# Decoder layer with a large expert table: PSUM banks, a DMA queue, buffers and the pace of the gate changed in the expert stage

## The chip, the cores and the metric

The kernel runs on one core of a Trainium2 chip, in one launch. The metric is the time of an execution on the device in microseconds (us), as the median of several executions. A profile of one execution shows what each engine did: TensorE (PE; PEld is its weight load), VectorE (DVE), ScalarE (ACT), GpSimd (POOL), SyncE (SP), and the 16 DMA engines.

## The reference: what is computed

One decoder layer on 512 tokens of width 1024: an attention part with two kinds of heads, a LayerNorm, and an expert part ("PEER") with a second LayerNorm. The change is in the expert part alone. There each token has 8 heads; each head picks 16 of 16384 experts, whose up and down vectors are rows of two tables:

```python
def peer(h, w_pq, sub_keys, u_tab, v_tab):
    def chunk(hx):                                       # 128 tokens
        q = (hx @ w_pq).reshape(PEER_CHUNK, PEER_HEADS, 2, PEER_HALF)
        sc = jnp.einsum('thpd,hpnd->thpn', q, sub_keys)
        v_half, i_half = lax.top_k(sc, PEER_TOPK)        # 16 of 128, twice
        ...                                              # 256 sums of pairs
        top_s, top_pos = lax.top_k(cand, PEER_TOPK)
        idx = jnp.take_along_axis(cand_idx, top_pos, axis=-1)
        g = jax.nn.softmax(top_s, axis=-1)
        a = jax.nn.gelu(jnp.einsum('thkd,td->thk', u_tab[idx], hx), approximate=False)
        return jnp.einsum('thk,thkd->td', (g * a).astype(hx.dtype), v_tab[idx])
```

## The kernel before, in words

Tokens are in four tiles of 128. The attention part, the first LayerNorm and the scores for the selection fill the first 374 us or so; the change touches them only through the number of raw buffers.

The expert part mixes two ways of computing. **Gathered:** for tile 0 wholly, and for the up part of tile 1, GpSimd fetches the chosen rows with indirect DMAs (`fetch`, 512 KB each, 384 in all, six buffers `gb`), and VectorE multiplies and adds them (L748, L764). **Dense:** for the other tiles all 16384 experts are computed, in 128 blocks of 128 experts. `u_block(e)` makes the up activations of one block for 256 tokens: 512 KB of `u_T` into a raw buffer (`load_raw`, 3 buffers, SP's queue); for even e a split into two parts, `hi` on ScalarE (L82) and `lo` on VectorE (L83), and 24 matmuls; for odd e 8 matmuls from `raw` (L783); all into a PSUM bank `st`, of which there are two (L779). ScalarE then writes GELU(`st`) to a slot `a_r` of a ring (L790). The ring has NB + 1 = 33 slots.

Three stages follow each other:

- **Up stage.** `u_block(e)` for e = 0 to NB + NS - 1 = 103. The first NB = 32 activations stay in the ring. The next NS = 72 are stored to HBM by `keep` (a DMA `a_d<-a_r`, 128 KB, SP's queue), which frees their slot. Between the blocks stand the selection (`all_topk`, VectorE), gathers, and the gate (`all_g`, `make_g`): a weight for each token and expert, made from one-hot rows. One gate step is 16 one-hot products: 8 scalings on ScalarE (`go`, L683), 8 matmuls into two banks `acc` (L687), 2 copies to `stage` (L690); after two steps 1 MB goes to HBM (`g_d<-stage`). There are 48 steps; for each block GRATE = 0.62 of them are placed, the last 16 only when the gathers of tile 1 are done.
- **Up and down stage.** `v_block(n)` with `v_mm` is the down part: 512 KB of `v_blk`, split into `hi` and `lo`, times the activation weighted by the gate (`w`, `wh`, `wl`), 18 matmuls into six banks `acc`. Down blocks 0 to 23 alternate with the up blocks 104 to 127. Every eighth block `g_load` fetches 1.5 MB of gate for eight blocks (`gl`, two buffers, runs of 512 bytes), on SP's queue (L829).
- **Down stage.** Down blocks 24 to 127. The stored activations come last; each is read back (`a_b<-a_d`, two buffers, SP's queue).

Six PSUM banks `acc` and two `st` come from one pool from the up stage to the end. Instructions are placed in the engines' queues by a scheduler that goes by the order in the code, by the buffers that are free and by its own costs. Each queue is worked off in its order: an instruction that waits holds up all behind it, and SP's queue is the one that issues nearly all plain DMAs.

## Time and profile before

| | us |
|---|---|
| median of 3 executions (1716.8 to 1725.07) | 1720.55 |
| the profiled execution | 1716.91 |
| its span, first to last instruction | 1715.1 |
| TensorE busy (mean granted clock 0.935) | 1462.7 |
| VectorE busy | 1257.6 |
| ScalarE busy | 737.5 |
| GpSimd busy | 553.6 |

Busy times are unions over the span and overlap each other. The profile's transfers are 472.56 MB, 276 GB/s over the span: 269.82 MB on the one hardware queue (all issued by SP), 201.35 MB on the software queue (GpSimd's gathers). A share of DMA is the mean over the 16 engines.

### The profile page before, as it was taken

The numbers are of one execution on the slowest core, as the hardware profiler recorded it, in microseconds if no ns is written. First come the engines' busy times: TensorE is split into PE (matmuls) and PEld (weight loads), VectorE is DVE, ScalarE is ACT, GpSimd is POOL, SyncE is SP. The second block draws the span as 40 slices with busy tenths as digits, with TensorE's granted clock in tenths as the row PEclk, the third lists the DMA queues.
The fourth block names the chain that finished last, engine by engine and source line by source line (L and its number), as shares of the span: only waits on it lengthen the run. The fifth ranks groups of instructions, "written<-read, shape, count | busy, mean of one in ns | idle before, by whom it ended". The sixth has DMA issues, their size and how long they took to land.

```text
span 1715.1 us, 21754 instructions
## 1 busy us (share of the span) xinstructions
PE 1462.7 (85%) x7269; PEld 1226.5 (72%) x7269; DVE 1257.6 (73%) x2787; ACT 737.5 (43%) x1452; POOL 553.6 (32%) x402
## 2 busy tenths in 40 slices
PE   6999898997788789787878798799898778887997
PEld 5777687886677678676767686688676666665885
DVE  7787567999999777745666277567787677787867
ACT  2555534332377767662676421223333222332441
POOL 0000000005544343534344145343455345565000
PEclk9999899998899989998999999899899888998999
DMA  8765433227898899989898899898898999999852
GB/s 300 271 209 169 163 123 101 84 87 272 311 318 312 279 341 338 349 333 324 283 336 299 322 348 375 283 333 307 306 324 315 357 318 328 338 338 314 257 178 77
DMA packets 187042, 472.56 MB, mean 276 GB/s; under 512 B 15921, under 2 KB 84913, under 8 KB 183730
## 3 DMA queue, kind: packets, MB, share of 16 engines
q1 hardware_dynamic: 131634, 269.82, 46.2%
q0 software_dynamic: 55296, 201.35, 32.2%
q8 instruction: 57, 0.93, 0.2%
q14 instruction: 55, 0.45, 0.1%
HBM read 431.26 MB, written 39.85 MB: 275 GB/s over the span
## 4 chain that ended last, share of the span: by engine, by line
DMA 32%; PE 30%; DVE 17%; ACT 12%; issue 7%; SPq 1%; POOL 0%; DVEq 0%; ACTq 0%; POOLq 0%
DMA a_d<-a_r 11%; DMA raw<-v_blk 9%; DMA a_b<-a_d 6%; ACT go L683 4%; DVE acc L764 4%; PE bank L92 4%; PE bank L93 4%; PE bank L94 4%; PE st L783 4%; DMA raw<-u_T 3%; DVE lo L83 3%; PE acc L93 3%; PE acc L94 3%; PE acc L92 3%; ACT stage L690 2%
## 5 line engine op out<-in xcount | busy, mean ns | idle before, releaser
L734 POOL DMA_INDIRECT gb<-u_tab,ei x256 | 338.7, 1323 | 589.2 <-DVE gb L748 354.4
L83 DVE TENSOR_TENSOR lo<-raw,hi 128x1024 fp32r<-128x1024 f32 x211 | 257.5, 1221 | 216.8 <-ACT hi L82 213.1
L82 ACT CAST hi<-raw 128x1024 fp32r<-128x1024 f32 x211 | 220.8, 1048 | 379.1 <-DMA raw<-v_blk 217.5
L783 PE MATMUL st<-h2f,raw 128*128 128x256 f32 x1200 | 302.2, 405 | 79.0 <-ACT a_r L790 60.3
L92 PE MATMUL acc<-hi,wh 128*128 128x512 f32 x768 | 313.8, 409 | 39.3 <-ACT hi L82 35.1
L93 PE MATMUL acc<-lo,wh 128*128 128x512 f32 x768 | 311.6, 406 | 32.6 <-DVE lo L83 32.4
L783 PEld LDWEIGHTS st<-h2f,raw 128*128 128x128 f32 x1200 | 237.8, 204 | 120.9 <-ACT a_r L790 67.1
L748 DVE SCALAR_TENSOR_TENSOR gb<-gb,h2n 128x1024 f32<-128x1024 f32 x256 | 305.4, 1220 | 5.5 <-DMA gb<-u_tab,ei 3.6
L94 PE MATMUL acc<-hi,wl 128*128 128x512 f32 x768 | 308.3, 401 | 0.0
L734 POOL DMA_INDIRECT gb<-v_tab,ei x128 | 204.9, 1601 | 191.6 <-DVE acc L764 139.0
L92 PEld LDWEIGHTS acc<-hi,wh 128*128 128x128 f32 x768 | 150.2, 196 | 75.8 <-ACT hi L82 38.9
L93 PEld LDWEIGHTS acc<-lo,wh 128*128 128x128 f32 x768 | 150.1, 195 | 73.2 <-DVE lo L83 40.4
L94 PEld LDWEIGHTS acc<-hi,wl 128*128 128x128 f32 x768 | 150.0, 195 | 31.4
L683 ACT ACTIVATE go<-oh,iT 128x128 f32<-128x128 bf16 x384 | 167.6, 526 | 2.7 <-DVE oh L677 2.0
L92 PE MATMUL st<-h2h,hi 128*128 128x256 f32 x424 | 133.3, 314 | 35.1 <-ACT a_r L790 34.2
L764 DVE SCALAR_TENSOR_TENSOR acc<-gb,w,acc 128x1024 f32<-128x1024 f32 x127 | 162.5, 1279 | 0.0
L94 PE MATMUL st<-h2h,lo 128*128 128x256 f32 x424 | 130.3, 307 | 12.2 <-DVE lo L83 12.2
L100 POOL TENSOR_TENSOR rs_r<-rs_v,mhalf 128x1 f32<-128x1 f32 (+1 forms) x12 | 9.3, 775 | 373.5 <-DVE rs_v L98 319.2
L93 PE MATMUL st<-h2l,hi 128*128 128x256 f32 x424 | 126.8, 299 | 0.0
L92 PEld LDWEIGHTS st<-h2h,hi 128*128 128x128 f32 x424 | 88.3, 208 | 43.3 <-ACT a_r L790 41.1
L687 PE MATMUL acc<-go,oh 128*128 128x128 f32 x768 | 107.7, 287 | 7.0 <-ACT go L683 7.0
L687 PEld LDWEIGHTS acc<-go,oh 128*128 128x128 f32 x768 | 98.8, 195 | 16.1 <-ACT go L683 8.7
(212 smaller groups left out, 2090.6 us busy)
## 6 DMA issues: line engine op xcount, KB each, us to landing
raw<-u_T SPq DMA_DIRECT2D x128, 512.0 KB, 6.3
raw<-v_blk SPq DMA_DIRECT2D x128, 512.0 KB, 6.3
wada<-w_adaT SPq DMA_DIRECT2D x48, 512.0 KB, 4.5
g_d<-stage SPq DMA_DIRECT2D x24, 1024.0 KB, 7.1
gl<-g_d SPq DMA_DIRECT2D x16, 1536.0 KB, 15.2
a_d<-a_r SPq DMA_DIRECT2D x72, 128.0 KB, 4.9
a_b<-a_d SPq DMA_DIRECT2D x72, 128.0 KB, 5.1
raw<-w_pqT SPq DMA_DIRECT2D x16, 512.0 KB, 3.6
```

Of the source, the lines that this page charges most:

```text
L82: nc.scalar.copy(hi, src)
L83: split.last = nc.vector.tensor_sub(lo, src, hi.bitcast(F32))
L92: nc.tensor.matmul(ps, lh, rh, start=first, stop=False)
L93: nc.tensor.matmul(ps, lh, rl, start=False, stop=False)
L94: nc.tensor.matmul(ps, ll, rh, start=False, stop=last)
L683: nc.scalar.activation(go[:, i, :], oh0[:, :, i], AF.Copy, scale=iT[:, 2, t0 + i:t0 + i + 1])
L687: nc.tensor.matmul(ps[:, i * P:(i + 1) * P], oh1[:, 4 * u + i, :], go[:, 4 * u + i, :], start=True, stop=True)
L690: nc.scalar.copy(stage[:, :, w:w + 4].rearrange("p i t -> p t i"), ps.rearrange("p (t i) -> p t i", t=4))
L734: nc.gpsimd.indirect_dma_start(out=b, out_offset=None, in_=A[tab], in_offset=bass.IndirectOffsetOnAxis(ap=ei[:, j:j + 1], axis=0))
L748: paced(nc.vector.scalar_tensor_tensor(b, b, 1.0, h2n, op0=OP.mult, op1=OP.mult, accum_out=dots[:, j:j + 1]))
L764: paced(nc.vector.scalar_tensor_tensor(acc0, b, w[:, j:j + 1], acc0, op0=OP.mult, op1=OP.add))
L783: nc.tensor.matmul(ps, raw[:, k, :], h2f[:, k, :], start=k == 0, stop=k == KB - 1)
```

## The change

Five edits in one. While the up stage runs, the PSUM pool has four banks `st` and four `acc`; after it that pool is closed, and a new one has two and six, as before. The gate load is issued on ScalarE's queue. Raw buffers are four instead of three, buffers for activations that are read back three instead of two. The ring keeps 24 activations instead of 32, so 80 are stored instead of 72 (the up stage still has 104 blocks). GRATE is 0.75.

```diff
-NB = 32
+NB = 24
 GB = 8
-NS = 72
-GRATE = 0.62
+NS = 80
+GRATE = 0.75
...
-        raw = stream.tile(shape, F32, name="raw", tag="raw", bufs=3)
+        raw = stream.tile(shape, F32, name="raw", tag="raw", bufs=4)
...
-    psB = ctx.enter_context(tc.tile_pool(name="psB", bufs=1, space=bass.MemoryType.PSUM, reuse_waits="tile"))
+    psB_stack = ExitStack()
+    psq = [psB_stack.enter_context(tc.tile_pool(name="psB", bufs=1, space=bass.MemoryType.PSUM, reuse_waits="tile")), 4, 4]
...
-        return psB.tile([P, 512], F32, name="acc", tag="acc", bufs=6)
+        return psq[0].tile([P, 512], F32, name="acc", tag="acc", bufs=psq[2])
...
-        ps = psB.tile([P, TU], F32, name="st", tag="st", bufs=2)
+        ps = psq[0].tile([P, TU], F32, name="st", tag="st", bufs=psq[1])
...
     sel_stack.close()
+    psB_stack.close()
+    psq[:] = ctx.enter_context(tc.tile_pool(name="psC", bufs=1, space=bass.MemoryType.PSUM, reuse_waits="tile")), 2, 6
...
-        dma(gl, g_d.rearrange("g p i t -> p g (i t)")[:, :, e * TG:(e + GB) * TG])
+        nc.scalar.dma_start(gl, g_d.rearrange("g p i t -> p g (i t)")[:, :, e * TG:(e + GB) * TG])
...
-            a = vp.tile([P, TU], F32, name="a_b", tag="a_b", bufs=2)
+            a = vp.tile([P, TU], F32, name="a_b", tag="a_b", bufs=3)
```

Where instructions move, at three places. The number behind a tile's name only tells tiles of one kind apart.

SP's queue around the store of block 60, which is `a_d28` before and `a_d36` now (the number counts the stores). Before, with `raw_6526` the weights of block 65:

```order
L88 DMA raw_6460<-u_T 128x1024
L694 DMA g_d_155<-stage_6215 128x2048
L795 DMA a_d28_111<-a_r_6321 128x256
L88 DMA raw_6526<-u_T 128x1024
L795 DMA a_d29_112<-a_r_6341 128x256
L88 DMA raw_6546<-u_T 128x1024
L795 DMA a_d30_113<-a_r_6407 128x256
```

Now, with `raw_6640` the weights of block 66 and `raw_6680` those of block 67:

```order
L88 DMA raw_6640<-u_T 128x1024
L796 DMA a_d36_119<-a_r_6467 128x256
L695 DMA g_d_163<-stage_6407 128x2048
L88 DMA raw_6680<-u_T 128x1024
L796 DMA a_d37_120<-a_r_6513 128x256
L88 DMA raw_6697<-u_T 128x1024
L796 DMA a_d38_121<-a_r_6553 128x256
```

Loads and stores alternate as before; the load ahead of a store is that of the sixth block after it instead of the fourth.

ScalarE's queue at the turn from the up stage to the down blocks. Before, with `a_r_8001` and `a_r_8130` the GELUs of blocks 100 and 103, `stage_8047` the last piece of the gate:

```order
L790 ACTIVATE a_r_8001<-st_7970 128x256
...
L790 ACTIVATE a_r_8110<-st_8079 128x256
L790 ACTIVATE a_r_8130<-st_8119 128x256
L690 COPY stage_8047<-acc_8146 128x4x128
L690 COPY stage_8047<-acc_8152 128x4x128
L82 CAST hi_8256<-raw_8254 128x1024
```

Now, with `a_r_8029`, `a_r_8095` and `a_r_8172` the GELUs of blocks 99, 100 and 103, `stage_7946` the last piece of the gate, `gl_8196` the first gate load:

```order
L791 ACTIVATE a_r_8029<-st_8018 128x256
L691 COPY stage_7946<-acc_8045 128x4x128
L691 COPY stage_7946<-acc_8051 128x4x128
L82 CAST hi_8222<-raw_8220 128x1024
L791 ACTIVATE a_r_8095<-st_8064 128x256
L832 DMA gl_8196<-g_d_163 128x24x128
L791 ACTIVATE a_r_8112<-st_8101 128x256
L82 CAST hi_8276<-raw_8274 128x1024
L832 DMA gl_8624<-g_d_163 128x24x128
L791 ACTIVATE a_r_8152<-st_8121 128x256
L791 ACTIVATE a_r_8172<-st_8161 128x256
```

The last copies of the gate have moved ahead by four GELUs, and the first two gate loads stand between the GELUs.

The sixth gate load (for down blocks 40 to 47). Before, in SP's queue, between weights of down blocks; `raw_9805` is that of down block 33:

```order
L88 DMA raw_9728<-v_blk 128x1024
L88 DMA raw_9770<-v_blk 128x1024
L829 DMA gl_10062<-g_d_155 128x24x128
L88 DMA raw_9805<-v_blk 128x1024
L88 DMA raw_9843<-v_blk 128x1024
```

Now, in ScalarE's queue, with `gl_9480` and `gl_9780` the gates of the blocks before:

```order
L855 CAST wh_9756<-gl_9480 128x128
L856 CAST wh_9756<-w_9754 128x256
L82 CAST hi_9712<-raw_9710 128x1024
L832 DMA gl_10082<-g_d_163 128x24x128
L82 CAST hi_9750<-raw_9748 128x1024
L855 CAST wh_9798<-gl_9780 128x128
```

It stands behind the last cast that reads the gate in its own buffer, `gl_9480`, and ahead of the cast of the next block's weights; SP's queue holds only weights there.

## Rows read from the trace of the kernel before

**Rows 1.** Stages: busy us (instructions) of PE, PEld, DVE, ACT, POOL; clock, DMA share, GB/s.

```profile
374.00:541.00 167.00, 136.78 (x769) 120.77 (x769) 154.19 (x485) 89.31 (x148) 74.63 (x55) 0.91 0.79 286
541.00:976.00 435.00, 344.18 (x2082) 309.94 (x2081) 277.63 (x434) 271.62 (x515) 180.26 (x133) 0.93 0.89 321
976.00:1182.00 206.00, 184.21 (x793) 153.79 (x792) 129.93 (x241) 46.80 (x102) 80.39 (x67) 0.94 0.95 330
1182.00:1592.00 410.00, 343.29 (x1385) 273.58 (x1384) 316.14 (x450) 123.99 (x232) 208.31 (x130) 0.90 0.93 324
```

**Rows 2.** The page's chain that ended last, by line, share of the span.

```profile
DMA a_d<-a_r 11%; DMA raw<-v_blk 9%; DMA a_b<-a_d 6%; ACT go L683 4%; DVE acc L764 4%; PE bank L92 4%; PE bank L93 4%; PE bank L94 4%; PE st L783 4%; DMA raw<-u_T 3%; DVE lo L83 3%; PE acc L93 3%; PE acc L94 3%; PE acc L92 3%; ACT stage L690 2%
```

**Rows 3.** Stores `a_d`, 541 to 976 us: issues, who waited, issue to landing.

```profile
L795 SPq DMA_DIRECT2D a_d<-a_r x72: 319/320/434, 541.8 to 969.2; - x72
...
  ACT a_r L790: 93.1, 37
...
DMA to landing us min/median/max: 1.7/4.9/9.9
```

**Rows 4.** Waits, 541 to 976 us: who for whom, us, times, longest.

```profile
PE st L783 <- ACT a_r L790: 56.9, 25, 4.8
PE st L92 <- ACT a_r L790: 28.0, 14, 6.6
...
ACT hi L82 <- DMA raw<-u_T: 47.6, 18, 6.4
```

**Rows 5.** Timeline of SP and ScalarE: start, us, what [idle before <-releaser].

```profile
701.73 0.32 SPq L795 DMA_DIRECT2D a_d<-a_r  x1
...
707.94 0.38 ACT L790 ACTIVATE a_r<-st 128x256 f32<-128x256 f32 x1 [5.28 <-DMA a_d<-a_r]
```

**Rows 6.** Up stage for tile `go` (PE, PEld, ACT), then `acc` (PE, PEld, DVE, ACT).

```profile
541.00:976.00 435.00, 86.79 (x640) 81.22 (x640) 137.74 (x316) 0.93 0.89 321
...
541.00:976.00 435.00, 87.94 (x646) 82.03 (x646) 0.00 (x0) 81.72 (x84) 0.93 0.89 321
```

**Rows 7.** Timeline of SP and TensorE at the turn to the down blocks.

```profile
971.56 0.33 SPq L694 DMA_DIRECT2D g_d<-stage  x1
...
986.47 0.80 PE L92 MATMUL acc<-hi,wh 128*128 128x512 f32 x1 [3.66 <-ACT wh L852]
```

**Rows 8.** Timeline of SP, ScalarE and TensorE around one gate load.

```profile
1201.72 0.38 SPq L829 DMA_DIRECT2D gl<-g_d  x1
1204.39 33.81 SPq L88 DMA_DIRECT2D raw<-v_blk  x7
...
1223.54 1.04 ACT L82 CAST hi<-raw 128x1024 fp32r<-128x1024 f32 x1 [12.69 <-DMA raw<-v_blk]
...
1224.64 0.80 PE L92 MATMUL acc<-hi,wh 128*128 128x512 f32 x1 [6.04 <-ACT hi L82]
```

**Rows 9.** Waits of TensorE, 1182 to 1592 us, then 976 to 1182 us.

```profile
PE acc L92 <- ACT hi L82: 35.1, 8, 8.9
PE acc L93 <- DVE lo L83: 31.6, 17, 10.0
...
PE st L783 <- DMA raw<-u_T: 17.4, 3, 9.6
```

**Rows 10.** The page's DMA issues: KB each, median us to landing.

```profile
raw<-u_T SPq DMA_DIRECT2D x128, 512.0 KB, 6.3
raw<-v_blk SPq DMA_DIRECT2D x128, 512.0 KB, 6.3
...
gl<-g_d SPq DMA_DIRECT2D x16, 1536.0 KB, 15.2
```

**Rows 11.** DMA from 1182 to 1592 us, and a 50 us window (columns of rows 1).

```profile
DMA packets 65422, 132.89 MB, mean 324 GB/s; under 512 B 4320, under 2 KB 37984, under 8 KB 65400
...
1050.00:1100.00 50.00, 44.03 (x196) 36.49 (x194) 32.89 (x61) 9.20 (x21) 22.52 (x20) 0.98 0.98 354
```

**Rows 12.** Waits of SP's queue over the span, at the gate loads.

```profile
SPq L829 <- DVE wl L854: 10.3, 5, 4.1
```

## The prediction

> **What bounds the kernel now.** I read the stages first: a table of windows cut where the work changes [rows 1]. From 374 to 541 us up blocks 0 to 31 run beside the selection and VectorE is busy 154 of 167 us. From 541 to 976 us (blocks 32 to 103, each with its store) no engine is full: TensorE 344 of 435 us, VectorE 278, ScalarE 272; the transfer engines are busy 0.89. From 976 to 1182 us 24 up blocks and 24 down blocks alternate (0.95). From 1182 to 1592 us only down blocks run, TensorE is busy 343 of 410 us, transfers 0.93. The rest is bound by TensorE and isn't touched.
>
> Then the chain of waits: its longest entry is the store of an up block's activation, 11% of the span, next the down block's weights, 9% [rows 2]. The 72 stores start from 541.8 to 969.2 us [rows 3], one each (969.2 - 541.8)/71 = 6.02 us. Why: the ring has one slot more than the blocks that it keeps, so the GELU of a block waits until the store before it has landed. The store issued at 701.73 holds the GELU at 707.94, which had been idle 5.28 us [rows 5]. A landing takes 4.9 us in the median [rows 3]; with 0.39 us for the GELU and 0.1 us of hand-overs the chain alone would run at **5.4 us**. The missing 0.6 us is a GELU that comes late though its slot is free. TensorE in turn waits for the GELU to free one of its two banks, 56.9 + 28.0 = 85 us [rows 4].
>
> In the last two stages I look for what TensorE waits for. At 1224.64 us it had been idle 6.04 us for a cast, and the cast 12.69 us for its block's weights. That load was issued at 1204.39 us, on SP's queue right behind the gate load of 1201.72 us [rows 8]. A gate load takes 15.2 us, a block of weights 6.3 [rows 10]. One gate load serves eight blocks. TensorE's waits for the two halves of the weights add up to 35.1 + 31.6 = **67 us** from 1182 to 1592, and 17.4 us in three waits for up weights before that [rows 9].
>
> **The change part by part.** The sum is made against the profiled execution, 1716.9 us, 3.6 us under the median of three; the difference is taken off the median.
>
> *Up stage.* Four banks instead of two let TensorE work up to four blocks ahead of the GELU. They do not shorten the store chain: 24 activations are kept in 25 slots, so there is still one spare. What can go is the 0.6 us of lateness, at most 71 x (6.02 - 5.4) = 44 us; at least nothing goes. Where the GELU is late, ScalarE is mostly busy with the gate: 316 scalings for 137.7 us and about 80 copies for 81.7 us [rows 6]. That is 8 x 0.436 + 2 x 1.0 = 5.5 us for each gate step. With 0.62 steps a block ScalarE has 0.62 x 5.5 + 0.4 + 0.5 = 4.3 us of work a block (0.4 the GELU, 0.5 half of a 1.04 us cast [rows 8], due in every second block), with 0.75 it has 5.0. Blocks with gate work I therefore leave at 6.0. But the first 32 gate steps end sooner: in the order, their last copy stands by the GELU of block 70 before and of block 60 now. Blocks 61 to 79 then carry no gate work: 19 x 0.6 = 12 us. The fourth raw buffer takes a part of the 47.6 us for which ScalarE waits for up weights [rows 4]; some of that wait lies beside the store chain, so I take a sixth, 8 us. Together **-20**, range -44 to 0.
>
> *Eight blocks more in the store chain* (24 to 31). The 32 blocks of that stage took 167/32 = 5.2 us each [rows 1], the chain allows 5.4: up to 2 us. Eight stores and eight reads more are 2 MB, at 321 to 324 GB/s [rows 1] up to 6.5 us. VectorE is the bound where the faster gate steps begin, which I count with these. **+3**, range 0 to +8.
>
> *The turn to the down stage.* The last gate store goes out at 971.56 us; the first down matmul starts at 986.47 us after TensorE idled 3.66 us [rows 7]. In the new order the last gate copies stand behind block 99's GELU, not behind block 103's, and the first gate load right behind block 100's. So the load lands while up blocks still run. **-5**, range -9 to 0. ScalarE now waits there for the last gate store; behind it stand the GELUs of blocks 101 to 103, which wait for their own stores anyway.
>
> *Gate loads on ScalarE's queue, four raw buffers.* SP's queue loses the gate load, so a block's weights no longer stand behind 1.5 MB of it. The bytes remain. From 1182 to 1592 us 132.9 MB move at 324 GB/s, and the best stretch of the trace moves 354 [rows 11]: 132.9/0.354 = 375 us, so at most 35 of TensorE's 67 us can come back by transfers. VectorE takes the gathered rows in program order and will wait for them more when three queues share the engines. I take half, **-18**, range -35 to 0. In the stage before, transfers are at 0.95 already [rows 1]: half of the 17.4 us, **-8**, range -17 to 0.
>
> What the move adds: 16 issues on ScalarE, at the 0.38 us that SP needed for one [rows 8] 6 us, hidden in an engine that is busy 124 of 410 us [rows 1]. Each gate load from the third on also waits for VectorE to finish with the slot; queued behind it are the casts of the next two blocks' weights and, early on, a GELU. On SP such a wait cost 10.3 us in five cases, 4.1 at most [rows 12]. VectorE would wait for those casts. As its own next work is taken from gathers, I count nothing; uncovered it is 10 to 15 us. Four instead of six banks for the gate still hold two steps of two; the change of pool waits for one copy. Both nothing, 2 us at the most.
>
> The Trainium skill speaks against this part: "DMA: Bandwidth & Descriptors", section "Issuing engines are not separate DMA queues", says that transfers issued from different engines run on the same 16 engines and interleave, and that a second issuer saves only issue time. The same page's section "Queues, rings and completion order" says that each engine takes turns between the queues that have work. The trace agrees with the first on bandwidth (0.93 busy, [rows 1]); a wait of 12.69 us behind a gate load [rows 8] is what the second would remove. The kernel before has all its hardware transfers on one queue, so its trace can't show two side by side.
>
> Sum: -20 + 3 - 5 - 18 - 8 = **-48**, so 1716.9 - 48 = 1669 against the profile and 1720.5 - 48 = **1672** as a median.
>
> **The rivals.**
> 1. *The move of the gate loads gives nothing*, because the transfers are work-bound: what the weights gain, gathers and gate loads lose, and the 26 us of the last two parts stay. For it: 0.93 and 0.95 busy [rows 1]. Against: 324 GB/s beside 354 [rows 11]. 1672 + 26 = 1698. The skill's first rule would come out here.
> 2. *The ring still sets the pace of every block.* Landings lengthen as more is in flight, and blocks stay at 6.0 us with or without gate work. The 20 us go: 1692.
> 3. *Neither does what it says*: 1 and 2 together leave 1716 to 1720, no change.
> 4. *Slower, by the store chain.* With four buffers SP issues a block's weights just ahead of the store; in the new order each store stands behind a load of the block five or six later. If a store then lands with such a load, at 6.3 us [rows 10] instead of 4.9, a block takes 6.3 + 0.5 = 6.8 us, and 80 blocks 544 us, where 72 x 6.02 + 8 x 5.2 = 475 are spent now: +69. The other terms give back 28: 1761. It decides from a median landing of (475 + 28)/80 - 0.5 = 5.8 us. For it: landings reach 9.9 us [rows 3]. Against: now, too, a load stands between two stores, and it was issued behind the first of them.
> 5. *More than forecast*: all of the lateness and what the transfers allow: -44 - 9 - 35 - 17 = -105 at the very most, 1616; a likely one is 1630.
>
> **How the numbers follow.** Forecast 0.52 (1648 to 1688), rival 1 0.12, rival 2 0.12, rival 3 0.08, rival 4 0.07, rival 5 0.09. The range 1640 to 1712 leaves out rival 4, the upper half of rival 3 and most of rival 5. A measurement of this kernel can tell about 0.5% from no change, here 8.6 us: faster than 1712 are the forecast and rivals 1, 2 and 5, 0.85; within it 0.08; slower 0.07.
>
> **What would show it.** Up stage right: stores of blocks 61 to 79 at about 5.4 us, TensorE's wait for the GELU near zero, the GELU's wait for the store larger than 93.1 us [rows 3] since nothing else is late. A median landing over 5.8 us is rival 4, one about 5.5 rival 2. Gate loads right: no cast of weights idles over 8 us behind a gate load, TensorE's 67 us fall to 40 or less, and the transfers of that stage pass 335 GB/s; TensorE's waits unchanged with longer gathers is rival 1. Wrong would also be: ScalarE idle at its gate loads for several us each with VectorE waiting for casts.

## The result: 1661.7 us, and the profile after

| | us | ratio to before | 95% interval |
|---|---|---|---|
| before, beside it on the same chip | 1718.7 (1712.8 to 1725.1) | 1 | |
| after | 1661.7 (1661.1 to 1668.7) | 0.9677 | 0.9633 to 0.9722 |
| after, once more beside the second group of experiments | 1667.8 (1664.8 to 1671.9) | 0.9697 | 0.9657 to 0.9738 |

The profiled execution of after has a span of 1659.3 us, 55.8 less than before. The forecast was 1672, in a range of 1640 to 1712. Its total is 10 us off. Its terms are much further off, and in both directions, as the stages show: that they cancel to 10 us is luck. Each stage runs from the start of one instruction in the trace to the start of another. Stages of every kernel in this document, in us (the names of edited kernels begin with b for before and a for after; each stands below with its edit):

| kernel | start to GELU 0 | up blocks 0 to 31 | up blocks 31 to 103 | GELU 103 to first down matmul | down blocks 0 to 23 (with up 104 to 127) | down blocks 24 to 101 | from down block 102 | span |
|---|---|---|---|---|---|---|---|---|
| before | 374.0 | 160.2 | 434.5 | 17.7 | 195.2 | 414.8 | 118.6 | 1715.1 |
| after | 370.0 | 168.0 | 439.8 | 0.6 | 189.1 | 366.7 | 125.0 | 1659.3 |
| a_again | 368.6 | 176.4 | 438.7 | 0.6 | 191.8 | 367.8 | 126.2 | 1670.1 |
| b_gl | 374.0 | 157.5 | 441.6 | 19.0 | 190.0 | 381.0 | 127.4 | 1690.5 |
| b_raw4k24 | 367.5 | 168.7 | 434.3 | 19.1 | 192.1 | 404.9 | 117.1 | 1703.8 |
| a_glsp | 368.2 | 168.5 | 438.4 | -0.5 | 199.2 | 393.0 | 117.1 | 1683.9 |
| a_raw3 | 369.8 | 185.1 | 444.2 | 0.6 | 201.3 | 376.9 | 124.6 | 1702.5 |
| a_st2 | 369.5 | 169.2 | 445.2 | 0.6 | 199.6 | 370.0 | 124.0 | 1678.2 |
| a_gr62 | 369.0 | 163.6 | 424.1 | 21.1 | 185.6 | 369.8 | 124.3 | 1657.5 |
| a_ring29 | 367.4 | 163.4 | 408.7 | 1.8 | 196.0 | 370.7 | 123.8 | 1631.7 |
| a_spread | 366.2 | 167.5 | 440.0 | 0.6 | 199.8 | 390.8 | 119.1 | 1684.1 |
| a_ab4 | 368.8 | 167.6 | 447.5 | 0.6 | 191.4 | 360.7 | 122.5 | 1659.2 |
| a_best4 | 366.4 | 163.7 | 407.0 | 5.6 | 190.8 | 359.3 | 123.6 | 1616.4 |
| a_half | 368.9 | 170.3 | 443.0 | 0.6 | 192.0 | 322.1 | 123.9 | 1621.0 |

How far one profile carries shows in the lines of after and a_again, which are the same kernel: 8.4 us apart in up blocks 0 to 31, under 3 in every other stage.

What was expected of the second run:

> The kernel after once more, unedited, on the chip of the three kernels below, so that differences of 10 us can be read: 0.964 to 0.972 of the kernel before.

The windows of after, cut at these milestones (columns as in [rows 1]: length, busy time of PE, PEld, DVE, ACT and POOL, granted clock, DMA share, GB/s):

```profile
369.99:538.02 168.03, 135.90 (x776) 121.10 (x776) 152.77 (x474) 94.81 (x159) 76.00 (x54) 0.91 0.79 285
538.02:977.86 439.84, 349.24 (x2064) 312.52 (x2062) 280.94 (x449) 265.33 (x504) 182.26 (x133) 0.90 0.90 323
978.48:1167.56 189.08, 182.25 (x801) 151.53 (x801) 130.70 (x240) 45.91 (x102) 84.47 (x68) 0.99 0.96 344
1167.56:1534.28 366.72, 332.13 (x1405) 270.16 (x1404) 314.29 (x446) 123.39 (x232) 192.47 (x130) 0.95 1.00 364
1534.28:1659.30 125.02, 109.74 (x469) 88.47 (x467) 87.04 (x154) 38.67 (x73) 2.19 (x4) 0.95 0.55 174
```

Beside [rows 1] the up stage is where it was: the same length, transfers at 0.90 instead of 0.89. The down stage is another one: transfers 1.00 instead of 0.93, 364 GB/s instead of 324.

The page of after says the same of the whole. First what the queues moved (q1 is SP's, q10 ScalarE's, q0 the gathers), then the first entries of the chain of waits:

```profile
q1 hardware_dynamic: 84530, 246.76, 41.8%
q0 software_dynamic: 55296, 201.35, 32.9%
q10 hardware_dynamic: 49408, 25.17, 5.4%
...
DMA 40%; PE 27%; DVE 16%; ACT 11%; issue 5%; SPq 0%; POOL 0%; ACTq 0%; DVEq 0%; POOLq 0%
DMA gl<-g_d 15%; DMA a_d<-a_r 11%; DMA raw<-v_blk 6%; ACT go L684 4%; PE bank L92 4%; PE bank L93 4%; PE bank L94 4%; DVE lo L83 3%; DMA raw<-u_T 3%; DVE gb L749 3%; PE acc L93 3%; PE acc L92 3%; PE acc L94 3%; ACT stage L691 2%; PE st L784 2%
```

The store `a_d<-a_r` keeps the 11% that it had in [rows 2]. The gate load is now the longest entry, 15%. The trace of after gives no landing times of single transfers, so the landing of a store (4.9 us in [rows 3]) can't be compared.

Waits in the up stage of after (window 541 to 978; total us, times, longest), to be held against [rows 3] and [rows 4]:

```profile
ACT a_r L791 <- DMA a_d<-a_r: 123.4, 42, 9.3
...
ACT hi L82 <- DMA raw<-u_T: 28.7, 18, 5.1
...
PE st L784 <- ACT a_r L791: 22.4, 10, 4.7
...
PE st L92 <- ACT a_r L791: 14.6, 5, 5.3
```

TensorE's wait for a bank fell from 85 to 37 us, and ScalarE's wait for the store rose from 93.1 to 123.4. The wait has moved from one engine to the other, and the stage is as long as before.

Waits of VectorE, TensorE and ScalarE in the down stage of after (window 1167 to 1534):

```profile
DVE w L851 <- DMA a_b<-a_d: 47.7, 9, 8.7
...
PE acc L93 <- DVE lo L83: 23.1, 9, 7.4
ACT hi L82 <- DMA raw<-v_blk: 18.0, 7, 10.7
...
PE acc L92 <- ACT hi L82: 11.5, 2, 6.8
```

Those of SP's queue in the same window:

```profile
SPq L847 <- DMA gl<-g_d: 85.4, 5, 19.5
...
SPq L88 <- DMA gl<-g_d: 51.3, 4, 22.1
```

The waits that ScalarE's queue executes at the line of the gate load (count, shortest, median and longest in ns, first and last start in us):

```profile
L832 ACTq EVENT_SEMAPHORE  x14: 17/17/1336, 961.7 to 1566.7; - x14
```

TensorE's 67 us of [rows 9] are 23.1 + 11.5 = 35. They are hardly waits for weights any more: every stall of TensorE over 1.5 us in this window, 30 us in all, follows a wait of VectorE's `w` for an activation that is read back (`a_b<-a_d`), behind which `lo` stands in VectorE's queue. ScalarE doesn't stand at its gate loads: 1.3 us at the longest. But SP now waits up to 22 us for a gate load that it didn't issue. All plain transfers in this trace take eight completion semaphores in turn (a semaphore is the counter that tells of a transfer's end), so one on SP's queue that takes the semaphore of the gate load waits until that has ended. The gate load issued at 1380.62 us and the transfer that SP issued at 1415.98 share one. In the nine such waits the gate load ends 29 to 38 us after its issue, against 15.2 in [rows 10].

### The profile page after: what moved, and what is told of

It reads as the page before. It is cut to its first block, busy times and chain, and to the rows that moved or that the text cites. A ratio compares the mean times of both kernels' runs of the same rounds, so it can differ in the third digit from the quotient of the medians.

```text
span 1659.3 us, 21831 instructions
## 1 busy us (share of the span) xinstructions
PE 1450.2 (87%) x7269; PEld 1221.7 (74%) x7269; DVE 1258.0 (76%) x2787; ACT 735.5 (44%) x1452; POOL 545.2 (33%) x402
## 4 chain that ended last, share of the span: by engine, by line
DMA 40%; PE 27%; DVE 16%; ACT 11%; issue 5%; SPq 0%; POOL 0%; ACTq 0%; DVEq 0%; POOLq 0%
DMA gl<-g_d 15%; DMA a_d<-a_r 11%; DMA raw<-v_blk 6%; ACT go L684 4%; PE bank L92 4%; PE bank L93 4%; PE bank L94 4%; DVE lo L83 3%; DMA raw<-u_T 3%; DVE gb L749 3%; PE acc L93 3%; PE acc L92 3%; PE acc L94 3%; ACT stage L691 2%; PE st L784 2%
## 5 line engine op out<-in xcount | busy, mean ns | idle before, releaser
L735 POOL DMA_INDIRECT gb<-u_tab,ei x256 | 344.9, 1347 | 570.4 <-DVE gb L749 352.4
L83 DVE TENSOR_TENSOR lo<-raw,hi 128x1024 fp32r<-128x1024 f32 x211 | 257.7, 1222 | 195.1 <-ACT hi L82 189.1
L784 PE MATMUL st<-h2f,raw 128*128 128x256 f32 x1200 | 298.4, 400 | 51.1 <-ACT a_r L791 39.9
L93 PE MATMUL acc<-lo,wh 128*128 128x512 f32 x768 | 306.6, 399 | 28.0 <-DVE lo L83 28.0
L92 PE MATMUL acc<-hi,wh 128*128 128x512 f32 x768 | 309.1, 402 | 22.8 <-ACT hi L82 11.5
L94 PE MATMUL acc<-hi,wl 128*128 128x512 f32 x768 | 304.2, 396 | 0.0
L784 PEld LDWEIGHTS st<-h2f,raw 128*128 128x128 f32 x1200 | 233.3, 201 | 90.1 <-ACT a_r L791 46.7
L735 POOL DMA_INDIRECT gb<-v_tab,ei x128 | 190.3, 1487 | 166.4 <-DVE acc L765 156.2
L93 PEld LDWEIGHTS acc<-lo,wh 128*128 128x128 f32 x768 | 147.5, 192 | 64.3 <-DVE lo L83 33.5
L92 PEld LDWEIGHTS acc<-hi,wh 128*128 128x128 f32 x768 | 147.5, 192 | 55.8 <-ACT hi L82 12.6
L688 PE MATMUL acc<-go,oh 128*128 128x128 f32 x768 | 126.1, 308 | 39.2 <-ACT go L684 16.9
L688 PEld LDWEIGHTS acc<-go,oh 128*128 128x128 f32 x768 | 111.0, 208 | 57.0 <-ACT go L684 44.7
L92 PE MATMUL st<-h2h,hi 128*128 128x256 f32 x424 | 132.1, 312 | 18.1 <-ACT a_r L791 16.7
L856 ACT CAST wh<-w 128x256 fp32r<-128x256 f32 x128 | 51.7, 405 | 179.9 <-DVE w L851 175.8
```

What stands on the lines that cost most here:

```text
L83: split.last = nc.vector.tensor_sub(lo, src, hi.bitcast(F32))
L92: nc.tensor.matmul(ps, lh, rh, start=first, stop=False)
L93: nc.tensor.matmul(ps, lh, rl, start=False, stop=False)
L94: nc.tensor.matmul(ps, ll, rh, start=False, stop=last)
L688: nc.tensor.matmul(ps[:, i * P:(i + 1) * P], oh1[:, 4 * u + i, :], go[:, 4 * u + i, :], start=True, stop=True)
L735: nc.gpsimd.indirect_dma_start(out=b, out_offset=None, in_=A[tab], in_offset=bass.IndirectOffsetOnAxis(ap=ei[:, j:j + 1], axis=0))
```

## The experiments

Theory A: the gate loads' own queue makes the down stage shorter. Theory B: the additional buffers do it. For the up stage: the ring's one spare slot sets the pace (rival 2), against transfers that set it. For what is left in the down stage: theory S, SP's waits for long gate loads, against theory T, the bytes.

**The queue alone.** The kernel before with one edit:

```diff
-        dma(gl, g_d.rearrange("g p i t -> p g (i t)")[:, :, e * TG:(e + GB) * TG])
+        nc.scalar.dma_start(gl, g_d.rearrange("g p i t -> p g (i t)")[:, :, e * TG:(e + GB) * TG])
```

> The kernel before with one edit of the five: the gate load is issued on ScalarE's queue. Theory A (the move of the gate loads alone makes the down stage shorter, because a block's weights no longer stand behind 1.5 MB in SP's queue): most of the 48 us by which the down stage became shorter come with this edit, 1680 to 1692 us, the stage from 1182 us on shorter by 25 to 45 us, TensorE's waits for the two halves of the weights under 45 us instead of 67. Theory B (the fourth raw buffer and the third buffer for read-back activations do it, the queue only saves issue time): within 8 us of before, 1710 to 1725 us, waits as before.

Measured: 1697.6 us, 0.9895 (0.9842 to 0.9948). Its window of down blocks 24 to 101:

```profile
1182.05:1563.10 381.05, 338.70 (x1406) 274.10 (x1404) 312.66 (x443) 125.50 (x232) 197.49 (x130) 0.94 0.96 348
```

That stage is 33.8 us shorter, by the queue alone, which is theory A's 25 to 45. The whole gained only 15 us, and ended 6 us above theory A's 1692: up blocks 31 to 103 took 7 us more, the part from down block 102 on 9 more. The last cost shows in nearly every kernel with the gate load on ScalarE's queue (122 to 127 us there, a_spread apart) against 117 to 119 with it on SP's; what makes it is open. "DMA: Bandwidth & Descriptors" of the Trainium skill, section "Issuing engines are not separate DMA queues", would leave only issue time to be saved. Here it is 33.8 us of 414.8 in that stage, with the same bytes. What a load no longer stands behind counts too.

**The queue undone.** The kernel after with this edit:

```diff
-        nc.scalar.dma_start(gl, g_d.rearrange("g p i t -> p g (i t)")[:, :, e * TG:(e + GB) * TG])
+        dma(gl, g_d.rearrange("g p i t -> p g (i t)")[:, :, e * TG:(e + GB) * TG])
```

> The kernel after with the gate load back on SP's queue, all else as after. Theory A (the queue does it): the gain falls to that of the turn and a little, 1695 to 1710 us, and casts of weights idle over 8 us behind a gate load again. Theory B (the buffers do it): within 8 us of after, 1655 to 1670 us.

Measured: 1688.3 us, 0.9844 (0.9789 to 0.9900). Undoing the queue costs 0.0147 to 0.0167 of 1718, 25 to 29 us, 26 of them in down blocks 24 to 101 (393.0 instead of 366.7). That lies between the two theories: the other edits do part of it without the queue (393.0 instead of 414.8 in before).

**The buffer alone, and undone.** The fourth raw buffer needs 4 KB, and the kernel before has no room for it beside 33 slots. So this one is the kernel before with

```diff
-NB = 32
+NB = 24
...
-NS = 72
+NS = 80
...
-        raw = stream.tile(shape, F32, name="raw", tag="raw", bufs=3)
+        raw = stream.tile(shape, F32, name="raw", tag="raw", bufs=4)
```

> The kernel before with two of the edits: four raw buffers, and 24 kept activations with 80 stored, which makes the room for the fourth. Gate loads on SP's queue, 0.62 gate steps a block, two banks for up blocks as before. The kernel after without its fourth buffer lost 45 us, so the buffer is worth most of the gain there. If it is worth that by itself: 1675 to 1690 us. If it is worth it only together with the gate loads on their own queue (before with the queue alone 15 us, after with the queue undone 27 us lost): 1695 to 1712 us. If eight more stored activations eat it: 1712 to 1725.

Measured: 1703.4 us, 0.9907 (0.9880 to 0.9935), the middle case: down blocks 24 to 101 are 9.9 us shorter, the start 6.5, and up blocks 0 to 31 longer by 8.5, about what two runs of one kernel can differ there. In that down stage the casts hardly wait for their weights any more (16.2 us instead of 93.4 in before), yet TensorE waits 50.9 us for `lo` and 10.5 for `hi`, 61 instead of 67: VectorE's `w` waits 75.3 us for activations that are read back, which stand in SP's queue too. No run changes the third buffer for those by itself; a_glsp, which has it, is 11.9 us shorter in this stage than b_raw4k24, with the banks and the gate's pace changed as well.

Now the kernel after with

```diff
-        raw = stream.tile(shape, F32, name="raw", tag="raw", bufs=4)
+        raw = stream.tile(shape, F32, name="raw", tag="raw", bufs=3)
```

> The kernel after with three raw buffers instead of four. The gate loads moved alone gave 15 us (ratio 0.9895); moved back in the kernel after they cost about 27. If the fourth raw buffer is what makes the queue worth more (the load of a block can be issued a block earlier, so that a gate load beside it does no harm): 10 to 20 us slower than the unedited kernel after, most of it from 1163 us on. If the third buffer for read-back activations does it: within 6 us, with the down stage at 367 us as it is.

Measured: 1712.7 us, 0.9964 (0.9937 to 0.9991). Going back to three buffers costs 46 to 49 us, more than twice what I expected, and only 9 to 10 of that in down blocks 24 to 101, where I expected most of it. By the table: 9 to 17 us in up blocks 0 to 31, 4 to 6 in the blocks up to 103, 10 to 12 in down blocks 0 to 23, 9 to 10 in down blocks 24 to 101. That makes 32 to 43 of them; its profiled run is 8.5 us under its median. Three windows of it (up blocks 0 to 31, down blocks 0 to 23, down blocks 24 to 101):

```profile
369.80:554.93 185.13, 144.99 (x779) 126.01 (x777) 150.52 (x463) 94.08 (x158) 73.27 (x53) 0.89 0.72 258
...
999.74:1201.04 201.30, 188.81 (x800) 153.64 (x801) 129.93 (x238) 45.45 (x100) 83.62 (x67) 0.97 0.93 327
1201.04:1577.91 376.87, 337.67 (x1406) 270.92 (x1404) 312.83 (x443) 124.78 (x232) 179.43 (x130) 0.95 0.99 356
```

And a wait in the last of them:

```profile
ACT hi L82 <- DMA raw<-v_blk: 138.7, 46, 12.2
```

In blocks 0 to 31 the same bytes take longer, at 258 instead of 285 GB/s; which wait does that, the runs don't show. Casts of down weights wait 138.7 us instead of 18.0 in after. Alone the two edits gave 15 and 14 us. In the kernel after, taking the queue away costs 25 to 29 and taking the buffer away 46 to 49: each is worth more with the rest of the edits there. That it is the other one of the two that does this is likely, but no run has just these two.

**The four banks.** The kernel after with

```diff
-    psq = [psB_stack.enter_context(tc.tile_pool(name="psB", bufs=1, space=bass.MemoryType.PSUM, reuse_waits="tile")), 4, 4]
+    psq = [psB_stack.enter_context(tc.tile_pool(name="psB", bufs=1, space=bass.MemoryType.PSUM, reuse_waits="tile")), 2, 6]
```

> The kernel after with two banks for up blocks and six for the gate while the up stage runs, as before; all else as after. If the ring with its single spare slot paces the up blocks, the four banks only move a wait from TensorE to the queue ahead of ScalarE: the time stays within 6 us of after (1656 to 1668 us), with TensorE's waits for the GELU back at about 85 us instead of 37. If the four banks bought time that something else in the up stage gave back, 10 to 25 us slower than after (1672 to 1687).

Measured: 1677.6 us, 0.9770 (0.9716 to 0.9824), some 13 to 16 us slower than after, in intervals that still touch. That is the second of the two cases that I expected, not the first. By the table about 6 lie in up blocks 31 to 103 and 8 to 10 in down blocks 0 to 23; why the second, the runs don't show. Two of its waits in the up stage:

```profile
ACT a_r L791 <- DMA a_d<-a_r: 124.3, 40, 7.4
...
PE st L784 <- ACT a_r L791: 62.1, 24, 5.7
```

TensorE waits 62.1 us for a bank at the odd blocks again instead of 22.4, and the GELU's wait for the store is the same 124. In the up stage the banks moved a wait; as a gain of the whole they are uncertain.

**The gate's pace.** The kernel after with

```diff
-GRATE = 0.75
+GRATE = 0.62
```

> The kernel after with 0.62 gate steps for each block instead of 0.75. By my reading the faster gate moves work within the up stage and takes the last gate copies off the turn: 5 to 15 us slower than the unedited kernel after, lost between the last GELU and the first down matmul (0.6 us in after, 17.7 in before). If the gate's pace is without effect on the end: within 5 us. If the faster gate costs the up stage more than it gives at the turn: up to 10 us faster.

Measured: 1667.4 us, 0.9711 (0.9668 to 0.9753), the same as after: the second case, and not the 5 to 15 us that my own reading gave. Two windows of it, up blocks 31 to 103 and from the last GELU to the first down matmul:

```profile
532.64:956.73 424.09, 352.30 (x2082) 316.63 (x2082) 279.94 (x442) 270.71 (x517) 183.30 (x133) 0.91 0.90 329
956.73:977.81 21.08, 10.09 (x32) 8.08 (x33) 2.80 (x4) 3.80 (x7) 0.00 (x0) 0.67 0.93 297
```

Up blocks 31 to 103 are 15.7 us shorter and up blocks 0 to 31 4.4, the turn is 20.5 us longer, and the first down matmul starts at 977.81 us against 978.48 in after. The gate's pace shifts work between the two and moves nothing behind them.

**Spare slots in the ring.** The kernel after with

```diff
-        a = ring.tile([P, TU], F32, name="a_r", tag="a_r", bufs=NB + 1)
+        a = ring.tile([P, TU], F32, name="a_r", tag="a_r", bufs=NB + 5)
```

> The kernel after with 29 slots for up activations instead of 25; 24 are still kept, so five are spare instead of one. If the store chain (a GELU waits for the landing of the store just before it) paces the up stage, the stage from 541 us to the last GELU falls from 437 us to what its work and transfers ask, 370 to 400 us, and the kernel to 1610 to 1645 us, with the GELU's waits for stores under 20 us instead of 123. If transfers pace it (0.90 of the engines' time in that stage), the waits go to other places and the time stays within 10 us of after (1651 to 1671).

Measured: 1630.8 us, 0.9494 (0.9441 to 0.9547), 31 to 35 us better than after. Its window of up blocks 31 to 103:

```profile
530.70:939.36 408.66, 338.99 (x2068) 305.49 (x2068) 285.30 (x464) 264.27 (x510) 190.34 (x135) 0.92 0.94 349
```

The largest wait of ScalarE there (541 to 939):

```profile
ACT hi L82 <- DMA raw<-u_T: 108.0, 23, 10.8
```

Four more slots take 31 us out of this stage. The GELU's wait for a store, 123.4 us in after, is gone from the list. What comes next is the load of the weights, 108.0 us, with transfers at 0.94 and 349 GB/s. I take that for the reason why the stage stopped at 409 and not in the 370 to 400 that I expected; no run tests it.

**The gate load in pieces.** The kernel after, with 192 KB of the next eight blocks' gate fetched at each down block (`g_new` makes the buffer, `g_part` issues the load of some of its 24 pieces on ScalarE's queue):

```diff
...
         if order[n] % GB == 0:
-            gl = g_load(order[n])
+            if n == 0:
+                gl = g_new()
+                g_part(gl, order[0], 0, NTG)
+            else:
+                gl = nxt
+            nxt = g_new() if n + GB < NKEY else None
+        if nxt is not None:
+            i = n % GB
+            g_part(nxt, order[n - i + GB], i * NTG // GB, (i + 1) * NTG // GB)
```

> The kernel after with the gate load of 1.5 MB cut into eight loads of 192 KB (three of the 24 pieces of the gate each), of which one is issued for each down block, for the next group of eight, on ScalarE's queue as in after. Theory S (the stalls that are left in the down stage, five to ten us each near down blocks 53, 62, 71, 79, 87 and 95, come because SP's next loads wait up to 22 us for the end of a long gate load on the other queue): SP's waits for gate loads fall from 85 us to under 15, the stalls go, and the down stage from 24 to 101 becomes 20 to 40 us shorter than 367, the kernel 15 to 40 us faster than the unedited one. Theory T (the transfers bound that stage, busy 1.00, at 363 GB/s): the bytes are the same, the waits move to the casts' loads, and the time stays within 8 us.

Measured: 1687.3 us, 0.9819 (0.9776 to 0.9862): 20 us slower than after, foreseen by neither theory. Waits of ScalarE, and behind them those of SP's queue, in down blocks 24 to 101:

```profile
ACT hi L82 <- DMA gl<-g_d: 40.7, 5, 8.9
ACT wh L856 <- DMA gl<-g_d: 37.0, 7, 11.4
...
SPq L88 <- DMA gl<-g_d: 46.5, 14, 8.9
SPq L848 <- DMA gl<-g_d: 27.9, 6, 7.4
```

SP waits 74 us instead of 137, but in 20 places instead of nine, and ScalarE now waits too, 78 us instead of 5, with the casts of the weights behind it. The edit doesn't tell S from T: each piece takes a semaphore of the eight, so a semaphore comes round sooner than before, and it is shared by both queues.

**Fewer loads between gate loads.** The kernel after, with stored activations read back four at a time:

```diff
...
-            a = vp.tile([P, TU], F32, name="a_b", tag="a_b", bufs=3)
-            dma(a, a_d[e - NB])
+            if (e - NB) % 4 == 0:
+                back[0] = vp.tile([P, 4, TU], F32, name="a_b", tag="a_b", bufs=2)
+                dma(back[0], a_d[(e - NB) // 4].rearrange("b p t -> p b t"))
+            a = back[0][:, (e - NB) % 4]
...
```

> The kernel after with the stored activations read back four at a time (one load of 512 KB for four blocks instead of four of 128 KB; the same bytes, in runs of the same length). The two tiles for it need 5 KB more, so two of the last constants go to a buffer that is no longer read. It changes how many loads SP issues between two gate loads: 10 instead of 16. Eight completion semaphores are used in turn by all plain loads, so the eighth load behind a gate load waits for its end: after four blocks now, after six and a half in this kernel. In the kernel after no block between 24 and 47 is late, where nothing is read back and that wait comes after eight blocks. Theory S (that wait makes the stalls from block 53 on): SP's waits for gate loads fall from 51 to 87 us to under 25, the stalls of 6 to 14 us near blocks 53, 62, 79, 87, 95 go, the kernel is 15 to 30 us faster than after. Theory T (traffic: from block 48 on 128 KB more are read for each block): stalls at the same places with other names, within 8 us of after.

Measured: 1662.2 us, 0.9687 (0.9627 to 0.9748), as after. Its window of down blocks 24 to 101:

```profile
1175.96:1536.67 360.71, 332.45 (x1405) 269.75 (x1404) 314.25 (x446) 123.41 (x232) 189.56 (x130) 0.95 1.01 373
```

SP's wait for gate loads in it (1167 to 1534):

```profile
SPq L88 <- DMA gl<-g_d: 127.6, 9, 26.6
```

My reckoning of the waits failed: they are 127.6 us and not under 25. SP stands later, as reckoned (behind the gate load that goes out beside block 75, it waits at block 81 and no longer at 79), but that gate load takes 43 us instead of 35. So this run doesn't remove what it was to remove. Yet the stage is 6 us shorter: it doesn't pay for the length of SP's waits as such.

**Half of the gathers left out.** The kernel after with

```diff
-            b = fetch("v_tab", ei, j)
+            b = b if j % 2 else fetch("v_tab", ei, j)
```

> The kernel after, but of the 128 gathered fetches of down rows for tile 0 every second one is left out; VectorE works the previous row's buffer off a second time, so that all other engines do what they did (tile 0's expert part is not the reference's). 33.5 MB less move in the down stage (down blocks 24 to 101), of 133. Theory T (the transfers bound that stage of the kernel after: share 1.00, 360 to 376 GB/s): the blocks run at the 4.08 us that TensorE needs, 78 of them take 318 to 332 us instead of 367, and the kernel becomes 35 to 50 us faster than the unedited one (1664). Theory S (SP's waits for the end of a long gate load, not the bytes, make the stalls from block 53 on): the gate loads and the order of the eight semaphores are as before, the stalls stay, at least 355 us, within 12 us of the unedited kernel.

Measured: 1622.1 us, 0.9447 (0.9400 to 0.9495). Its down blocks 24 to 101:

```profile
1174.97:1497.07 322.10, 319.85 (x1405) 263.03 (x1404) 312.98 (x446) 123.20 (x233) 101.34 (x66) 1.00 0.93 317
```

With 33.5 MB less the stage takes 322.1 us and TensorE is busy 319.9 of them, as theory T has it. SP's waits for gate loads fall too, to 18.1 + 16.7 us, so this run alone doesn't exclude S, and a_ab4, whose waits stayed, doesn't either. It does show that TensorE can run the stage in 322 us once these transfers are gone. How much of it S can be at most, the pauses below show.

**The version that beats both.** a_ring29 and a_ab4 in one kernel:

> The two edits that aim at what is left in the kernel after, together: five spare slots in the ring for up activations (31 us alone), and stored activations read back four at a time. Theory S: the gains add, 0.930 to 0.942 of the kernel before, 1597 to 1618 us. Theory T: as with the spare slots alone, 0.945 to 0.955.

Measured: 1618.6 us, 0.9422 (0.9379 to 0.9466), 44 to 47 us better than after. Its down blocks 24 to 101:

```profile
1133.52:1492.81 359.29, 330.23 (x1405) 268.51 (x1404) 313.40 (x446) 122.49 (x231) 194.54 (x130) 0.96 1.01 374
```

Most of it is the ring; reading back by fours adds about 11 us to a_ring29 in this stage, and on the whole 12 us, in intervals that overlap. That is just short of what theory S gave and more than theory T did. SP's wait for gate loads is as long as in a_ab4, so it isn't S's mechanism; what the row shows is that the same bytes move at 374 GB/s instead of a_ring29's 361.

**Where transfers pause.** I cut down blocks 24 to 101 of each kernel into slices of 4 us and counted those with a DMA share under 0.9: before 27 of 103, b_raw4k24 20 of 101, b_gl 19 of 95, a_glsp 19 of 98, a_raw3 14 of 94, after 9 of 91, a_ab4 6 of 90, a_best4 4 of 89. A full slice, one with 0.98 or more, shows a share of 1.04 in the mean. Four slices of before, over one pause:

```profile
1297.71:1301.71 4.00, 3.53 (x16) 2.60 (x14) 0.00 (x0) 0.00 (x0) 0.40 (x1) 1.00 1.04 392
1301.71:1305.71 4.00, 0.00 (x0) 0.00 (x0) 0.00 (x0) 0.35 (x1) 0.00 (x0) 1.00 0.94 373
1305.71:1309.71 4.00, 2.79 (x6) 1.90 (x7) 3.28 (x4) 2.83 (x7) 0.58 (x1) 0.52 0.28 75
1309.71:1313.71 4.00, 4.00 (x13) 3.15 (x12) 4.00 (x7) 0.86 (x1) 2.42 (x3) 0.62 0.75 232
```

In the timeline of before, the same microseconds (start, length, instruction, idle time before it, other lines left out):

```profile
1305.36 1.04 ACT L82 CAST hi<-raw 128x1024 fp32r<-128x1024 f32 x1 [11.86 <-DMA raw<-v_blk]
...
1306.43 1.23 DVE L83 TENSOR_TENSOR lo<-raw,hi 128x1024 fp32r<-128x1024 f32 x1 [9.14 <-ACT hi L82]
...
1306.81 1.04 ACT L82 CAST hi<-raw 128x1024 fp32r<-128x1024 f32 x1
...
1307.69 4.39 SPq L88 DMA_DIRECT2D raw<-v_blk  x2
```

First TensorE, VectorE and ScalarE run dry while the transfers are full. Then the weights of two blocks are there at once, the next load goes out only when `lo`, the last reader of the first of their buffers, has ended (1306.43 + 1.23), at 1307.69, and the transfers pause until it does. In after such a pause is left where SP stood at the end of a gate load:

```profile
1407.56:1411.56 4.00, 4.00 (x19) 3.33 (x18) 2.04 (x3) 0.00 (x0) 2.60 (x2) 1.00 1.09 369
1411.56:1415.56 4.00, 2.06 (x10) 1.36 (x8) 0.00 (x0) 0.00 (x0) 0.00 (x0) 1.00 0.75 288
1415.56:1419.56 4.00, 0.00 (x0) 0.00 (x0) 1.56 (x3) 0.60 (x2) 0.00 (x0) 0.91 0.59 170
1419.56:1423.56 4.00, 2.55 (x6) 2.09 (x7) 4.00 (x8) 1.90 (x3) 1.94 (x2) 0.50 1.06 339
```

SP's queue issued the load of down block 78 at 1396.09 us and, after the wait, a read-back and the load of block 79:

```profile
1396.09 0.33 SPq L88 DMA_DIRECT2D raw<-v_blk  x1
1415.98 0.33 SPq L847 DMA_DIRECT2D a_b<-a_d  x1
1416.40 0.38 SPq L88 DMA_DIRECT2D raw<-v_blk  x1
```

Most of those 20 us were filled by the gate load and the gathers; the pause is what S is worth. Summed as what each such slice lacks to 1.04, an estimate, pauses cost 39 us in before and 11 in after. By this estimate S can be 11 us of after's 367 at most, and the rest is T's. The pauses are 28 of the 48 us by which this stage became shorter. The rate of full slices, 371 GB/s in before and 384 in after, makes some 13 more, by an estimate from 134 MB. It is 383 in b_gl and 375 in b_raw4k24, so most of that comes with the second queue; why, no run shows. In up blocks 31 to 103 the same count gives 48 us in before, 46 in after and 26 in a_ring29.

## Why the prediction held in its total and not in its terms

| step of the forecast | forecast | measured (table of stages) |
|---|---|---|
| up stage and eight more stored blocks (from GELU 0 to GELU 103) | -17 | +13.1 |
| the turn to the down stage | -5 | -17.1 |
| down blocks 0 to 23 | -8 | -6.1 |
| down stage, blocks 24 to 101 | -18 | -48.1 |
| start, and from down block 102 on | 0 | -4.0 and +6.4 |
| sum | -48 | -55.8 |

*The up stage failed, by 30 us.* The step "blocks with gate work I therefore leave at 6.0" was wrong. Blocks 32 to 60 took 6.40 us in before, above the mean of 6.02 that I used, and 6.71 in after; a_gr62, with the old pace, has 6.33. The faster gate takes from each such block what it gives back in blocks 61 to 79 (5.14 instead of 5.67 us). Those came a little lower than my 5.4. I had booked them against 6.02, though blocks 70 to 77 carried no gate work in before either: the 32nd step's last copy starts at 774.1 us, beside the GELU of block 70, the 33rd's first scaling at 818.2, right behind that of block 77. They took 5.62 us each there. Then blocks 80 to 103, which I had left as they were, took 6.15 instead of 5.89. The mechanism named in rival 2, the ring's single spare slot, is what held the stage: a_ring29 shows 31 us for it. I had written that the banks "do not shorten the store chain", and still booked 20 us beside that chain, 12 for blocks without gate work and 8 for the fourth raw buffer. ScalarE's wait for up weights did fall, from 47.6 to 28.7 us, but its wait for the store grew by 30.

*The turn was right in kind, 12 us too small, and it isn't a gain of its own.* a_gr62 shows the first down matmul at the same time with either pace. Up stage and turn must be taken as one: with the 4.0 us of the start, the first down matmul comes 8.0 us earlier (2.2 in a_again), where I had 22.

*The down stage was right in the queue, 30 us too small, and had only one of two paths.* The queue does most of it (33.8 us alone) and the buffers complete it. I read TensorE's 31.6 us for `lo` [rows 9] as a wait for weights. Of these, 25.7 us are stalls that follow a wait of VectorE's `w` for an activation that is read back, and I counted nothing for the third buffer of those. Two numbers were wrong besides. VectorE's wait in before (window 1182 to 1596), and the row of before for this stage, cut as those of after:

```profile
DVE w L848 <- DMA a_b<-a_d: 67.3, 14, 12.6
...
1181.71:1596.46 414.75, 348.04 (x1405) 277.52 (x1404) 320.89 (x458) 126.13 (x237) 208.31 (x130) 0.91 0.93 323
```

I took half of the 35 us of TensorE's idle time that transfers could give back. Idle time fell by 32, from 414.75 - 348.04 = 66.7 to 366.72 - 332.13 = 34.6 us, nearly all of that bound. And TensorE's busy time fell by 16 us for the same matmuls, which I didn't count at all: its granted clock rose from 0.91 to 0.95 of that stage. The rows of the two pauses above show why: a slice that runs at full clock, then one in which TensorE is idle, then one at 0.5 to 0.6. A stall costs its own length and then matmuls at or near the lower level of 1.2 GHz for some microseconds. The best stretch of before, 354 GB/s in 50 us [rows 11], was also no limit: after holds 364 for 367 us, and full slices average 371 GB/s in before and 384 in after.

*What would show it.* TensorE's 67 us at 40 or less: 35. Transfers past 335 GB/s: 364. ScalarE idle at its gate loads: no. No cast idle over 8 us behind a gate load: not quite, 10.7 at the longest, but 18.0 us in all. TensorE's wait for the GELU near zero: 37. The GELU's wait for the store larger: 123.4. Blocks 61 to 79 at about 5.4: 5.14. The median landing, which was to tell rivals 2 and 4 apart, isn't in the trace of after.

*The rivals.* Rival 1 (the queue gives nothing) fell by b_gl. Rival 2 had the right mechanism for the up stage; its 1692 didn't come since the down stage gave more than I booked. Of rival 3 the range of 1640 to 1712 leaves out all of 1716 to 1720, and not only the upper half. Rival 4 (a store chain that costs 69 us) didn't come: a stored block of 32 to 103 takes 6.1 us, not 6.8. Rival 5's 1630 is what the kernel reaches once the ring has spare slots.

*What stays open.* What the third buffer for read-back activations gives by itself; why the part from down block 102 on costs 6 us more in after; why three raw buffers cost 9 to 17 us in up blocks 0 to 31 of after, when before has three and takes 160; why two banks cost 8 to 10 us in down blocks 0 to 23; and how much of the 11 us of pauses a gate load with a semaphore of its own would give back. No run settles these.

## What to carry to other kernels

Where transfers are the bound, count the slices in which they pause, and ask which queue stands still there and for what; here a queue of its own for the longest load and one more buffer were each worth more with the other edits than alone. A ring with one spare slot ties each producer to the landing of the transfer just before it: here four more slots gave 31 us. An engine's longest wait needn't be the one that holds the others: in b_raw4k24 the casts' wait for weights nearly went, and TensorE then waited for the read-back behind it. A shorter wait on one engine is no gain until the engine that it waited for is shown to be faster.

## What the runs showed of the hardware that I had not expected

- Two queues with the same bytes finish earlier than one: 414.8 to 381.0 us in down blocks 24 to 101, at 348 GB/s instead of 323, in the rows above.
- TensorE's stalls cost twice. The stage lost 32 us of idle time and 16 us of busy time with the same matmuls, at a granted clock of 0.95 instead of 0.91.
- A queue can wait for another queue's transfer that its program doesn't need: SP up to 26.6 us (a_ab4) for gate loads issued by ScalarE.
- One pause of 8 us in the up stage of after is no transfer's doing. SP's queue issued the store of an activation at 836.51 us and then nothing until 843.47, when the last copy into the gate's piece that it was to store (L691, 842.39 + 1.05) had ended; the row names a scaling beside that copy. The window, and then SP's wait from 825 to 850 us:

```profile
834.02:842.02 8.00, 8.00 (x42) 7.42 (x42) 6.09 (x9) 7.94 (x18) 2.13 (x2) 0.72 0.08 23
```

```profile
SPq L695 <- ACT go L684: 6.9, 1, 6.9
```

A store that is queued before its data exist holds up the loads behind it. Here transfers were at 0.08. TensorE was busy all 8 us, so what the pause costs isn't shown.
